# One-hot tiles of the gate stage: two tokens innermost instead of four

## The chip, the cores and the metric

The kernel runs on one core of one Trainium2 chip. The metric is the device time of one execution in microseconds (us), the median of several executions. Five engines work side by side: TensorE (PE, with its weight loads shown apart as PEld), VectorE (DVE), ScalarE (ACT), GpSimd (POOL), and SyncE (SP), which issues most of the DMAs.

## The reference

Two layers of a diffusion backbone over 256 latent and 256 context tokens of width 1024. Each layer has a mixer part (convolution, attention, Hyena, state space) and then an expert layer, PEER, in which every token picks 8 x 16 single-neuron experts out of 128 x 128. The change lies in the expert layer:

```
def peer(h, wq, sub_keys, u_tab, v_tab):
    def block(hb):                                   # 128 tokens
        q = (hb @ wq).reshape(128, 8, 2, 128)
        s = einsum('thpk,hpnk->thpn', q, sub_keys)
        v1, i1 = top_k(s[:, :, 0], 16)
        v2, i2 = top_k(s[:, :, 1], 16)
        cv, ci = top_k(all sums v1 + v2, 16)
        e = i1[ci // 16] * 128 + i2[ci % 16]         # (128, 128) expert numbers
        g = softmax(cv)                              # their gates
        act = gelu(einsum('td,ted->te', hb, u_tab[e]))
        return einsum('te,ted->td', g * act, v_tab[e])
```

## The kernel before

The expert layer is computed densely. All 16384 experts stand in 128 blocks of 128. For each block, `u_stage` (lines 1006 to 1019) loads 512 KB of `u`, splits it on ACT (`u_hi`, line 137) and on POOL or DVE (`u_lo`, line 138) into a rounded part and a rest, multiplies the two with the tokens on PE in 24 matmuls (`au`, lines 141 to 143), and ACT takes the gelu. Later the result is multiplied by gates and goes into the matmuls with `v` (`ov`). In layer 0 three tiles of 128 tokens go this dense way (so `au` has 384 columns) and a fourth is gathered; in layer 1 there are two (256 columns).

The gates come from the gate stage (lines 1170 to 1231). For a token it makes the 128 x 128 table of gates of all experts. The 128 slots of a token (8 heads x 16) lie on the partitions; `slots` brings the slot numbers and gates into that layout, 16 bit wide (`slT`). `hots` makes for a whole tile of 128 tokens the one-hot rows of the upper part of the first index (`o16[0]`, 16 wide), of its lower part (`o8`, 8 wide), and `o16[1]`, `o16[2]`, which are `o16[0]` times the high and the low part of the gate. `gates` then takes 16 tokens at a time (TB = 16, eight calls for a tile, called blocks below): three DVE operations of 2048 elements make `Ah` and `Al` (products of `o16` and `o8`, line 1206) and `B_` (one-hot of the second index, line 1209); two PE matmuls for each token, 128 x 128 x 128 in 16 bit, add `B_` x `Ah` and `B_` x `Al` in PSUM (`G`, lines 1215 and 1216); ACT copies four tokens at a time into `stg`; and SP writes the 16 tables, 1 MB, to DRAM (`Gd`).

In all these 16-bit tiles the last axis is a group of TC = 4 tokens. So `B_` is laid out as (group, 128 classes, 4 tokens), and the matmul of a token reads its 128 numbers at a step of TC elements:

```
o16 = [mk(tp, [128, NG, 16, TC], F16, tag=f"o16{j}", bufs=1) for j in range(3)]      # NG = 128 // TC
Ah = mk(tp, [128, ng, 128, TC], F16, tag="Ah", bufs=2)                               # ng = TB // TC
V.tensor_tensor(dst_.rearrange("p g (a b) c -> p g a b c", b=8), o16[j][:, gs_, :, None, :].to_broadcast(sh),
                o8[:, gs_, None, :, :].to_broadcast(sh), ALU.mult)
V.tensor_tensor(B_, iE[:, None].to_broadcast([128, ng, 128, TC]), ids_[:, :, None, :].to_broadcast([128, ng, 128, TC]), ALU.is_equal)
T.matmul(b[:, j * 128:(j + 1) * 128], B_[:, tt // TC, :, tt % TC], Ah[:, tt // TC, :, tt % TC], start=True, stop=False)
```

`iE` is a constant 0..127, each number TC times, loaded once for each layer. `Ah`, `Al` and `B_` have two buffers each, so the DVE work of block n+2 waits for the matmuls of block n.

Between the blocks PE does `u_stage`s ahead of need: in layer 0 after blocks 0, 2, 4, 6 and 7 of a tile, in layer 1 after every block; their `u_lo` runs on POOL. A scheduler places the instructions when the program is built; each engine then runs its own list in order. There are 24 blocks in layer 0 and 16 in layer 1.

Of the kernel before, what the change touches and what calls it, by code (L numbers as in the profile page):

```python
# [54 lines left out]
UEV = (0, 0)  # L55
GB = 8
TB = 16
TC = 4
GSC = 4096.0

SM = {}
# [22 lines left out]
def tile_hybrid_diffusion(ctx: ExitStack, tc: tile.TileContext, I: dict, out: bass.AP):  # L84
# [12 lines left out]
    def mk(p, shape, dt=F32, tag=None, name=None, **k):  # L97
        uid[0] += 1
        n = f"{name or tag}_{uid[0]}"
        if tag in SCR:  # L100
            k["bufs"] = SCR[tag]
        return p.tile(shape, dt, tag=tag or n, name=n, **k)
# [740 lines left out]
    for l in range(2):  # L843
# [177 lines left out]
        with ExitStack() as rt:  # L1021
# [139 lines left out]
            for t in GT:  # L1161
# [7 lines left out]
                gsl[t] = (eu, gd)  # L1169
            iE = mk(tp, [128, 128, TC], F16, tag="iE", bufs=1)  # L1170
            nc.sync.dma_start(iE, I["iotaE"])
# [10 lines left out]
            def hots(slT):  # L1182
                NG = 128 // TC

                def tv4(j, n):
                    return slT[:, j].rearrange("p (g c) -> p g c", c=TC)[:, :, None, :].to_broadcast([128, NG, n, TC])

                def ids(n):
                    return iE[:, None, 0:n, :].to_broadcast([128, NG, n, TC])
                o16 = [mk(tp, [128, NG, 16, TC], F16, tag=f"o16{j}", bufs=1) for j in range(3)]  # L1190
                o8 = mk(tp, [128, NG, 8, TC], F16, tag="o8", bufs=1)
                for dst_, n, j in ((o16[0], 16, 0), (o8, 8, 1)):
                    V.tensor_tensor(dst_, ids(n), tv4(j, n), ALU.is_equal)
                for j in range(2):
                    V.tensor_tensor(o16[1 + j], o16[0], tv4(3 + j, 16), ALU.mult)
                return slT, o16, o8
# [332 lines left out]
```

## Time and profile before

| | us |
|---|---|
| median of 3 runs | 2989.35 (2978.24 to 2992.91) |
| the profiled execution's own time | 2991.8 |
| its span, first to last instruction | 2990.0 |
| first matmul of the gate stage of layer 0 to its last, about | 652 to 807 |
| the same of layer 1, about | 2246 to 2352 |

PE is busy for 91% of the span, DVE for 69%, ACT for 39%, POOL for 25%. The gate stages take 261 us of the span. In the rows below a line of the trace has the start in us, the duration in us, the engine, the line of the program, the operation, output<-inputs with their shape, and, in brackets, the idle time of the engine before it and what ended that.

### The profile page before, as it was taken

What the parts mean: (1) busy time and instruction counts of PE and PEld (TensorE: products, weight loads), DVE (VectorE), ACT (ScalarE), POOL (GpSimd) and SP (SyncE); (2) the same over time, 40 slices, a digit from 0 to 9 for tenths busy, and PEclk for the clock granted to TensorE, in tenths of its full rate; (3) what the DMA queues carried; (4) which work ended last, traced back from release to release, by engine and by line L of the source; (5) the groups of instructions that cost most, each with busy time, mean ns of one, the idle gap of its engine ahead of it and who ended that gap; (6) DMA issues with size and microseconds to landing.
All of it is one profiled execution on the core that took longest, in us unless ns stands there. A gap on an engine that the chain in (4) does not pass through costs nothing.

```text
span 2990.0 us, 41926 instructions
## 1 busy us (share of the span) xinstructions
PE 2721.2 (91%) x15646; PEld 2352.7 (79%) x15646; DVE 2058.4 (69%) x4255; ACT 1179.0 (39%) x1810; POOL 754.3 (25%) x505
## 2 busy tenths in 40 slices
PE   6798879689999999999989998888779999999998
PEld 3674657489989988888878887666779999999986
DVE  4955449976487777777667646964997665555556
ACT  2233433235433333333333334334345544444443
POOL 2332013032224444444334103321563100000000
PEclk9899989889999999999999998898899999999999
DMA  7123434335699899889989645425336886666655
GB/s 257 56 90 101 140 113 144 128 111 217 230 340 317 312 321 317 305 311 310 310 288 310 215 127 171 129 71 190 113 119 212 288 271 214 217 202 215 203 183 197
DMA packets 241840, 625.21 MB, mean 209 GB/s; under 512 B 22424, under 2 KB 104794, under 8 KB 236004
## 3 DMA queue, kind: packets, MB, share of 16 engines
q1 hardware_dynamic: 201156, 475.18, 48.1%
q0 software_dynamic: 40480, 147.36, 14.0%
q8 instruction: 122, 2.00, 0.3%
q14 instruction: 82, 0.67, 0.1%
HBM read 573.17 MB, written 49.30 MB: 208 GB/s over the span
## 4 chain that ended last, share of the span: by engine, by line
PE 53%; DVE 17%; DMA 13%; issue 9%; POOL 5%; ACT 2%; SPq 0%; POOLq 0%; DVEq 0%; ACTq 0%
DMA grow<-in_vg_dram,eu 9%; PE ov L141 6%; PE ov L142 6%; PE ov L143 6%; PE au L141 5%; PE au L143 5%; PE au L142 5%; POOL grow L1311 4%; PE G L1215 3%; PE G L1216 3%; DVE yT L365 2%; PE pj L141 1%; DVE accg L1324 1%; PE pj L142 1%; PE pj L143 1%
## 5 line engine op out<-in xcount | busy, mean ns | idle before, releaser
L141 PE MATMUL au<-hT,u_hi 128*128 128x384 f32 (+1 forms) x2048 | 642.5, 314 | 3.6 <-ACT u_hi L137 3.6
L143 PE MATMUL au<-hT,u_lo 128*128 128x384 f32 (+1 forms) x2048 | 639.7, 313 | 4.5 <-POOL u_lo L138 3.2
L142 PE MATMUL au<-hT,u_hi 128*128 128x384 f32 (+1 forms) x2048 | 638.9, 312 | 0.0
L142 PE MATMUL ov<-v_lo,wh 128*128 128x512 f32 x1280 | 506.0, 395 | 32.7 <-DVE v_lo L138 32.6
L143 PE MATMUL ov<-v_hi,wl 128*128 128x512 f32 x1280 | 500.7, 391 | 0.0
L141 PE MATMUL ov<-v_hi,wh 128*128 128x512 f32 x1280 | 463.5, 393 | 6.2 <-ACT wh L137 6.2
L137 ACT CAST u_hi<-u_raw 128x1024 fp32r<-128x1024 f32 x256 | 269.6, 1053 | 487.0 <-PE au L142 364.3
L141 PEld LDWEIGHTS au<-hT,u_hi 128*128 128x128 f32 x2048 | 392.5, 192 | 12.2 <-ACT u_hi L137 4.5
L142 PEld LDWEIGHTS au<-hT,u_hi 128*128 128x128 f32 x2048 | 391.8, 191 | 7.7
L143 PEld LDWEIGHTS au<-hT,u_lo 128*128 128x128 f32 x2048 | 391.0, 191 | 8.0 <-POOL u_lo L138 3.9
L138 DVE TENSOR_TENSOR v_lo<-v_raw,v_hi 128x1024 fp32r<-128x1024 f32 x255 | 313.0, 1228 | 79.6 <-ACT v_hi L137 79.5
L138 DVE TENSOR_TENSOR u_lo<-u_raw,u_hi 128x1024 fp32r<-128x1024 f32 x198 | 242.3, 1224 | 159.7 <-ACT u_hi L137 159.7
L137 ACT CAST v_hi<-v_raw 128x1024 fp32r<-128x1024 f32 x256 | 268.8, 1050 | 137.6 <-DMA v_raw<-in_v_dram 103.7
L142 PEld LDWEIGHTS ov<-v_lo,wh 128*128 128x128 f32 x1280 | 241.9, 189 | 89.4 <-DVE v_lo L138 45.5
L137 ACT CAST wh<-act 128x384 fp32r<-128x384 f32 (+1 forms) x256 | 117.4, 461 | 447.1 <-PE ov L142 446.1
L141 PEld LDWEIGHTS ov<-v_hi,wh 128*128 128x128 f32 x1280 | 242.4, 190 | 51.3 <-ACT wh L137 6.5
L143 PEld LDWEIGHTS ov<-v_hi,wl 128*128 128x128 f32 x1280 | 242.1, 189 | 49.9
L138 POOL TENSOR_TENSOR w_lo<-w_raw,w_hi 128x1024 fp32r<-128x1024 f32 (+1 forms) x72 | 177.8, 2478 | 252.7 <-ACT w_hi L137 221.8
L1311 POOL DMA_INDIRECT grow<-in_vg_dram,eu x128 | 175.0, 1367 | 230.2 <-DVE accg L1324 187.1
L1311 POOL DMA_INDIRECT grow<-in_ug_dram,eu x128 | 161.2, 1260 | 272.4 <-DVE grow L1315 222.1
L138 POOL TENSOR_TENSOR u_lo<-u_raw,u_hi 128x1024 fp32r<-128x1024 f32 x58 | 149.6, 2585 | 305.0 <-ACT u_hi L137 240.8
L1324 DVE SCALAR_TENSOR_TENSOR accg<-grow,ag,accg 128x1024 f32<-128x1024 f32 x127 | 163.0, 1283 | 83.0 <-DMA grow<-in_vg_dram,eu 82.5
(832 smaller groups left out, 4493.3 us busy)
## 6 DMA issues: line engine op xcount, KB each, us to landing
u_raw<-in_uT_dram SPq DMA_DIRECT2D x256, 512.0 KB
v_raw<-in_v_dram SPq DMA_DIRECT2D x256, 512.0 KB
Gd<-stg SPq DMA_DIRECT2D x40, 1024.0 KB
gt<-Gd SPq DMA_DIRECT2D x80, 512.0 KB
wa_raw<-in_w_ada_dram SPq DMA_DIRECT2D x76, 512.0 KB
w_raw<-in_w_in_t_dram SPq DMA_DIRECT2D x44, 512.0 KB
w_raw<-in_wq_dram SPq DMA_DIRECT2D x32, 512.0 KB
w_raw<-in_w_ada_dram SPq DMA_DIRECT2D x20, 512.0 KB
```

Of the source, the lines that this page charges most:

```text
L137: S.copy(hi, src)
L138: late["V" if eng in (None, V) else "G"] = (eng or V).tensor_tensor(lo, src, hi.bitcast(F32), ALU.subtract)
L141: T.matmul(o, lh, rh, start=first, stop=False)
L142: T.matmul(o, lh, rl, start=False, stop=False)
L143: return T.matmul(o, ll, rh, start=False, stop=last)
L365: V.scalar_tensor_tensor(uc, upad[:, m, :, j:j + 256], wj, uc, op0=ALU.mult, op1=ALU.add)
L1215: T.matmul(b[:, j * 128:(j + 1) * 128], B_[:, tt // TC, :, tt % TC], Ah[:, tt // TC, :, tt % TC], start=True, stop=False)
L1216: T.matmul(b[:, j * 128:(j + 1) * 128], B_[:, tt // TC, :, tt % TC], Al[:, tt // TC, :, tt % TC], start=False, stop=True)
L1311: nc.gpsimd.indirect_dma_start(out=r, out_offset=None, in_=I[tab], in_offset=bass.IndirectOffsetOnAxis(ap=eu[:, i:i + 1], axis=0))
L1324: V.scalar_tensor_tensor(accg, r, ag[:, i:i + 1], accg, op0=ALU.mult, op1=ALU.add)
```

## The change

One constant is set from 4 to 2:

```
-TC = 4
+TC = 2
```

With it the last axis of `iE`, `o16`, `o8`, `Ah`, `Al` and `B_` is 2 tokens long, and the axis of groups is twice as long: `Ah` goes from (4, 128, 4) to (8, 128, 2) in each partition. The number of instructions, their elements, the buffers and their bytes stay, but for `iE`, which is half as long (64 KB to load instead of 128 KB). The order of the instructions is the same on PE, DVE, ACT and POOL, and on SP but for the size of the two loads of `iE`. What changes is how the data lie: a matmul of the gate stage reads its 16-bit numbers 4 bytes apart instead of 8, both for the weights (`B_`) and for the moving side (`Ah`, `Al`); and a DVE operation that repeats tokens along an axis reads a run of 2 numbers (4 bytes) again and again, where it read a run of 4 (8 bytes).

## Rows read from the trace of the kernel before

**Rows 1.** Both gate stages: length, busy us (and count) of PE, PEld, DVE, ACT, POOL, clock, DMA.

```profile
652.00:807.00 155.00, 154.97 (x1138) 150.87 (x1138) 89.02 (x79) 79.44 (x132) 36.59 (x15) 1.00 0.59 212
2246.00:2352.00 106.00, 106.00 (x882) 104.45 (x882) 65.33 (x52) 57.13 (x96) 32.49 (x13) 0.98 0.64 222
```

**Rows 2.** PE in order of time, layer 1: a gate block, a `u_stage`, the next block.

```profile
2274.71 0.30 PE L1216 MATMUL G<-Al,B__3362_19163 128*128 128x128 f16 x1
...
2278.02 0.30 PE L1216 MATMUL G<-Al,B__3362_19163 128*128 128x128 f16 x1
...
2278.27 0.28 PE L142 MATMUL au<-hT,u_hi 128*128 128x256 f32 x1
...
2280.91 0.28 PE L143 MATMUL au<-hT,u_lo 128*128 128x256 f32 x1
2281.03 0.29 PE L1215 MATMUL G<-Ah,B__3375_19244 128*128 128x128 f16 x1
```

**Rows 3.** PE in order of time, layer 0: matmuls of a `u_stage`.

```profile
672.18 0.34 PE L142 MATMUL au<-hT,u_hi 128*128 128x384 f32 x1
...
673.40 0.34 PE L143 MATMUL au<-hT,u_lo 128*128 128x384 f32 x1
```

**Rows 4.** Weight loads and matmuls in order of time; last, all transposes of one line.

```profile
657.67 0.12 PEld L1215 LDWEIGHTS <-B__857_4886 128*128 128x128 f16 x1 [0.15 <-issue]
657.68 0.13 PEld L1216 LDWEIGHTS <-B__857_4886 128*128 128x128 f16 x1
...
671.43 0.30 PE L1216 MATMUL G<-Al,B__878_5015 128*128 128x128 f16 x1
671.54 0.62 PE L1175 MATMUL tr<-cm,sl 128*128 128x128 f32 x4
...
L789 PE MATMUL xT<-cm,grow x8: 270/272/273, 1797.2 to 1798.0; 128*128 128x128 f32 x8
```

**Rows 5.** POOL and DVE in order of time, layer 1, around one block.

```profile
2282.28 2.39 POOL L138 TENSOR_TENSOR u_lo<-u_raw,u_hi 128x1024 fp32r<-128x1024 f32 x1 [4.26 <-ACT u_hi L137]
...
2284.91 1.23 DVE L1206 TENSOR_TENSOR Ah<-o,o 128x2048 f16<-128x2048 f16 x1 [3.18 <-PE G L1215]
2286.06 1.22 DVE L1206 TENSOR_TENSOR Al<-o,o 128x2048 f16<-128x2048 f16 x1
2287.19 1.22 DVE L1209 TENSOR_TENSOR B__3401_19406<-iE,slT 128x2048 f16<-128x2048 f16 x1
```

**Rows 6.** POOL and DVE in order of time, layer 0, where both want to run.

```profile
635.83 3.06 POOL L138 TENSOR_TENSOR u_lo<-u_raw,u_hi 128x1024 fp32r<-128x1024 f32 x1 [2.02 <-ACT u_hi L137]
...
636.75 3.22 DVE L1209 TENSOR_TENSOR B__870_4967<-iE,slT 128x2048 f16<-128x2048 f16 x1
...
648.59 2.58 POOL L138 TENSOR_TENSOR u_lo<-u_raw,u_hi 128x1024 fp32r<-128x1024 f32 x1 [1.89 <-ACT u_hi L137]
...
648.84 3.41 DVE L1206 TENSOR_TENSOR Al<-o,o 128x2048 f16<-128x2048 f16 x1
```

**Rows 7.** Waits in layer 0's gate stage, then in layer 1's: total us, times, longest.

```profile
DVE Ah L1206 <- PE G L1215: 58.5, 20, 6.5
...
DVE Ah L1206 <- PE G L1215: 32.8, 11, 4.0
```

**Rows 8.** DVE in order of time: sums in 16 bit, runs of 8, 4, 2 elements.

```profile
487.67 0.67 DVE L1067 TENSOR_TENSOR e<-e 128x1024 f16<-128x1024 f16 x1
...
510.25 0.44 DVE L1067 TENSOR_TENSOR e<-e 128x512 f16<-128x512 f16 x1
...
511.64 0.43 DVE L1067 TENSOR_TENSOR e<-e 128x256 f16<-128x256 f16 x1
```

**Rows 9.** DVE products in 32 bit by line: duration ns min/median/max.

```profile
L618 DVE TENSOR_TENSOR t2k<-t2k,cbm x12: 665/693/831, 222.3 to 1993.9; 128x512 f32<-128x512 f32 x12
...
L619 DVE TENSOR_TENSOR t2k<-t2k,dt x12: 677/692/743, 223.2 to 1994.6; 128x512 f32<-128x512 f32 x12
```

**Rows 10.** The stretch behind the gate stage of layer 0, columns as in rows 1.

```profile
807.00:860.00 53.00, 46.77 (x237) 43.33 (x237) 39.19 (x109) 17.66 (x26) 11.64 (x9) 0.94 1.00 331
```

## Prediction

> **What bounds the kernel now.** I read the busy shares by stage first, then PE's instructions in order of time, then DVE and POOL in the same stretches. In both gate stages PE is busy from end to end, 154.97 of 155 us and 106 of 106, and DVE and POOL are not [rows 1]. DVE waits there for the gate matmuls that free its buffers, 58.5 and 32.8 us in all [rows 7]. So PE sets the length of both stages, and its work is of two kinds. A gate matmul follows the one before after 0.118 us: 28 steps from 2274.71 to 2278.02. An `au` matmul of 256 columns takes 0.120 us: 22 steps from 2278.27 to 2280.91 [rows 2]. One of 384 columns takes 0.174 us: 7 steps in 1.22 us [rows 3]. A block is thus 32 x 0.118 = 3.78 us of gate matmuls, and a `u_stage` 24 x 0.120 = 2.88 us in layer 1 and 24 x 0.174 = 4.18 us in layer 0. Layer 1 has 16 x (3.78 + 2.88) = 106.6 us, which is the stage; layer 0 has 24 x 3.78 + 15 x 4.18 = 153.4 us, which is nearly the stage.
>
> **The change on PE.** The reader should note that a gate matmul has 128 columns and takes as long as an `au` of 256. From 256 to 384 columns the price rises by 0.054 us, 0.42 ns a column, so 128 columns at that rate would cost 0.120 - 0.054 = 0.066 us. The weight load doesn't explain the rest: with PE just free, the second load of a block starts 0.01 us behind the first, and the transposes behind a block, which have loads of another kind, still start 0.11 us after the last gate matmul [rows 4]. It is the matmul itself that occupies the array for 0.118 us. What sets it apart from `au` is its moving side: 16-bit numbers 8 bytes apart, where `au` reads 32-bit numbers that touch, 4 bytes apart. The change puts the 16-bit numbers 4 bytes apart, at the very addresses that `au` reads at 0.42 ns a column. The trace shows no 16-bit matmul at another step, so the price has bounds: 0.066 us below, 0.118 us above, since the numbers only move closer together. A row between is the transposes of 128 columns in 32 bit, 0.11 us (8 starts from 1797.2 to 1798.0 [rows 4]), but those are another type of matmul. I take 0.066, because the addresses are those of `au`. That is 32 x 0.052 = 1.66 us less for a block, 40 us for 24 blocks and 27 us for 16: PE's own work would fall to 115 us and 79 us.
>
> [...]
>
> **DVE.** Its operations keep their elements. Today 2048 elements in 16 bit take 1.22 us and start 1.14 us apart [rows 5]. Two elements are done at a time there: 512 elements in 32 bit take 0.69 us [rows 9], so a 32-bit word costs about (1.22 - 0.69) / 512 = 1.04 ns, and 1024 words of two numbers each fit 1.22 us. After the change a run is exactly one such word, and one input repeats that word, up to 128 times, while the other input and the output stay contiguous. Two rows bound this. Line 619 repeats one 32-bit word 128 times over 512 elements and takes 0.692 us, as line 618, which repeats whole rows, takes 0.693 [rows 9]: repeating a word is free. Against it, line 1067 needs 0.44 us for 512 elements in runs of four and 0.43 us for 256 in runs of two [rows 8]: there runs of two go at half the rate. But in that line both inputs and the output jump after each run; here nothing jumps. I take 1.14 us as before and keep half the rate, 1.22 + 1024 x 1.04 ns = 2.28 us, 2.20 from start to start, for a rival.
>
> [...]
>
> **What is late next.** PE can't collect the whole 67 us, because DVE and POOL do not run their two-input operations at the same time. A POOL `u_lo` begins at 635.83 and lasts 3.06 us; a DVE operation begins at 636.75 and takes 3.22 us instead of 1.22; the same at 648.59 and 648.84 [rows 6]. DVE ended each time some 1.1 us behind POOL: it had waited for the whole of it. Today the two take turns without loss in layer 1: POOL runs from 2282.28 for 2.39 us, while PE does a block, and DVE's three operations follow at 2284.91, when the block ends and PE turns to `u_stage` [rows 5]. With shorter blocks the two stand in a row. Their sum in layer 0: DVE 89.0 us less 0.08 us of overlap for each of 79 records, 82.7, and POOL 36.6, together 119.3 us [rows 1]; behind the last DVE operation PE has still two blocks and a `u_stage`, 2 x 2.1 + 4.2 = 8.4 us. That is 127.7 us, above PE's 115, so the stage goes from 155 to about 128: **27.3 us** saved. In layer 1: 65.3 - 52 x 0.08 = 61.1, POOL 32.5, and 2 x 2.1 + 2.9 = 7.1 behind: 100.7 us, above PE's 79, so the stage goes from 106 to about 101: **5.3 us** saved. Some of the recorded DVE time is itself waiting for POOL, which makes these sums a little long; new stalls in changing over make them short. I leave both out.
>
> The rest costs nothing. ACT has 79.4 and 57.1 us in the stages [rows 1], under either sum. The DMAs move 212 GB/s there and would move 212 x 155 / 128 = 257, below the 331 GB/s of the next stretch [rows 10]. That stretch has its DMA share at 1.00, but it begins with loads of the gate tables, which must be written first, so it moves forward as a whole. The shorter load of `iE` lies ahead of its use. Sum: 2991.8 - 27.3 - 5.3 = 2959.2, say **2959 us**; against the median of 2989.35, which is 2.5 us below the profiled execution, that is 1.0% faster.
>
> **The rivals.** *PE's step stays at 0.118 us*, because the step of 8 bytes was not its cause. Then PE bounds the stages as now: 2990, give or take 5. For it speaks that no 16-bit row at another step exists. A weaker form of it is a step of 0.11, as in the transposes: 40 x 32 x 0.008 = 10 us saved, 2980. *DVE drops to half rate.* The place is the three operations of a block, the price 2.20 us for 1.14, a factor of 1.93: layer 0 then has 82.7 x 1.93 + 36.6 + 8.4 = 205 us for 155, layer 1 61.1 x 1.93 + 32.5 + 7.1 = 158 for 106, so 102 us more: 3094. [...] *DVE and POOL get out of each other's way* better than their sum says; then PE's own work bounds: 2991.8 - 67 = 2925. Against it stand the collisions of rows 6.
>
> **How the numbers follow.** A measurement of this kernel can tell about 0.5%, 15 us, from no change. Chances: the forecast, 2947 to 2972, 0.55; the step unchanged or nearly so, 2980 to 2995, 0.27; less collision, 2925 to 2945, 0.06; DVE slower, 3040 to 3100, 0.12. Faster by over 0.5% is the first and third, 0.61; within 0.5% the second, 0.27; slower the last, 0.12. The range runs from 2940 to 2996, which leaves out the slower case and most of the third; the forecast's own range is 2947 to 2972.
>
> **What would show it.** Right: starts of gate matmuls 0.066 us apart in a block (up to 0.08 changes little), DVE operations at 1.22 us, idle time of PE inside the gate stages that ends with `Ah`, `Al` or `B_`, more DVE records of 2 to 3.4 us beside a `u_lo`, stages of about 128 and 101 us, and everything behind them as long as before. Wrong: gate matmuls still 0.118 apart, or DVE operations of 1.9 us or more. A granted clock below the 1.00 and 0.98 of the stages [rows 1], brought by the new idle time of PE, would eat some of the gain.

## The result and the profile after

The changed kernel takes **2945.15 us** (median of 4 runs, 2932.18 to 2949.5), the kernel before beside it 2987.64 (4 runs, 2978.24 to 2992.91). The ratio is 0.9854 with a 95% interval of 0.9813 to 0.9895: 42.5 us or 1.5% faster, where 30 us were forecast. The time lies in the range on record, 2940 to 2996, and 2 us below the forecast's own range of 2947 to 2972. A second measurement against 13 runs of the kernel before (the first experiment below) gives 0.9853, from 0.983 to 0.9876.

The windows of both gate stages of after, in the columns of [rows 1]:

```profile
652.00:783.00 131.00, 114.30 (x1136) 109.66 (x1134) 108.20 (x79) 70.32 (x130) 56.20 (x15) 0.96 0.68 244
2214.50:2306.00 91.50, 80.17 (x879) 77.69 (x879) 85.33 (x52) 51.67 (x94) 35.91 (x13) 0.94 0.70 241
```

The stages went from 155 to 131 us and from 106 to 91.5. PE's busy time fell by 41 and 26 us, but PE is no longer busy from end to end: 17 and 11 us are idle. Its granted clock fell too, from 1.00 and 0.98 to 0.96 and 0.94. DVE and POOL together are recorded for 164 us in a stage of 131, against 126 in 155 before. Since no work was added to either, the growth of their records is waiting for one another.

PE in order of time in layer 1, at the place of [rows 2], a gate block, a `u_stage` and the next block:

```profile
2250.18 0.23 PE L1215 MATMUL G<-Ah,B__3388_19325 128*128 128x128 f16 x1 [0.66 <-DVE B__3388_19325 L1209]
...
2251.96 0.22 PE L1216 MATMUL G<-Al,B__3388_19325 128*128 128x128 f16 x1
...
2252.19 0.28 PE L142 MATMUL au<-hT,u_hi 128*128 128x256 f32 x1
...
2254.82 0.28 PE L143 MATMUL au<-hT,u_lo 128*128 128x256 f32 x1
2255.79 0.23 PE L1215 MATMUL G<-Ah,B__3401_19406 128*128 128x128 f16 x1 [0.68 <-DVE B__3401_19406 L1209]
```

From the first of the 32 gate matmuls to the last it is 1.78 us, 31 steps of **0.057 us**, where it was 0.118. The `au` matmuls are as before: 22 steps in 2.63 us. And both blocks now begin with a wait for DVE's `B_`, 0.66 and 0.68 us: PE waits for DVE where DVE waited for PE.

DVE, POOL, PE and ACT of after in order of time, where layer 0 goes from its second tile of tokens to its third (the record of 724.37 holds two operations):

```profile
720.96 1.21 DVE L1209 TENSOR_TENSOR B__1009_5800<-iE,slT 128x2048 f16<-128x2048 f16 x1
722.10 1.21 DVE L1206 TENSOR_TENSOR Ah<-o,o 128x2048 f16<-128x2048 f16 x1
...
724.37 18.84 POOL L138 TENSOR_TENSOR u_lo<-u_raw,u_hi 128x1024 fp32r<-128x1024 f32 x2 [6.87 <-ACT u_hi L137]
...
728.91 1.21 DVE L1195 TENSOR_TENSOR o<-o,slT 128x2048 f16<-128x2048 f16 x1
...
737.46 1.22 DVE L1209 TENSOR_TENSOR B__1060_6099<-iE,slT 128x2048 f16<-128x2048 f16 x1
...
740.93 0.69 PE L143 MATMUL au<-hT,u_lo 128*128 128x384 f32 x1 [6.74 <-POOL u_lo L138]
...
746.69 1.05 ACT L137 CAST u_hi<-u_raw 128x1024 fp32r<-128x1024 f32 x1 [11.46 <-PE au L142]
747.82 2.40 POOL L138 TENSOR_TENSOR u_lo<-u_raw,u_hi 128x1024 fp32r<-128x1024 f32 x1 [4.62 <-ACT u_hi L137]
750.78 1.23 DVE L1206 TENSOR_TENSOR Ah<-o,o 128x2048 f16<-128x2048 f16 x1 [12.10 <-PE G L1215]
```

DVE's operations last 1.21 us and start 1.14 us apart, as in [rows 5]: the one-word runs cost DVE nothing. The long POOL record is the new thing. DVE runs without a gap from 715 to 738.7 us, and two `u_lo` that take 2.4 us each when alone are recorded for 18.8: the first for 16.5, of which all but the last 2.2 lie beside DVE's run, the second for 2.4. In a1, the second measurement of this kernel, POOL's 15 records in the stage again hold 54.27 us, against 56.20 here and 36.59 before. An `au` matmul waits 6.7 us for the first of them. The gate blocks stand behind it in PE's order, so the buffers that they free come late, and DVE stands for 12.1 us. The collisions of [rows 6] went the other way, DVE waiting for POOL; here POOL waits for DVE.

The waits of after, in layer 0's gate stage and then in layer 1's, answering to [rows 7]:

```profile
DVE Ah L1206 <- PE G L1215: 20.4, 5, 12.1
PEld au L143 <- POOL u_lo L138: 7.0, 1, 7.0
PE au L143 <- POOL u_lo L138: 6.7, 1, 6.7
...
PE G L1215 <- DVE Ah L1206: 12.1, 2, 7.5
...
DVE Ah L1206 <- PE G L1215: 4.7, 2, 3.0
```

DVE's waits for a gate matmul fell from 58.5 to 20.4 and from 32.8 to 4.7 us, and 12.1 of the 20.4 is the one just shown. Of PE's 12.1 us of waiting for `Ah` in layer 1, 7.5 stand before the first gate matmul, in the kernel before as well.

**Where the 43 us are.** The table gives, for every kernel of this study, the time from the start of the first gate matmul to the start of the last in either stage, worked out from the traces, with the stretch between the stages and the tail behind the second. "Step" is the median distance of two gate matmuls' starts (in e9, where two distances alternate, the mean).

```
kernel                    time us   step us  layer 0  between  layer 1   tail
before                    2991.8*    0.118     154.4   1439.6    105.3  638.8
after                     2945.15    0.057     130.9   1431.8     91.1  640.9
a1  after, again          2945.54    0.057     131.1   1439.6     90.2  640.2
e1  weights in twos       2986.05    0.117     153.1   1434.6    104.5  639.6
e2  moving in twos        2959.98    0.060     132.6   1440.3     91.4  640.7
e3  eight tokens          3177.55    0.234     265.9   1428.9    186.8  642.2
e4  one token             3080.73    0.056     208.0   1433.8    137.0  639.7
e5  after, u_lo on DVE    2908.24    0.057     117.2   1428.3     78.5  640.0
e6  before, u_lo on DVE   2973.08    0.118     155.2   1414.2    105.4  639.1
e7  e5, lead-in on DVE    2904.09    0.057     113.6   1418.9     76.0  640.3
e8  6 bytes apart         2984.44    0.088     156.6   1427.0    107.8  640.5
e9  Ah 8, Al 4 apart      2947.82    0.088     132.2   1432.8     93.4  638.9
(* the profiled execution; elsewhere the median of several runs, and one run each for e1 to e4, e8 and e9;
the stages are those of the profiled execution everywhere)
```

In the first profile of after the stages give 23.5 and 14.2 us and the stretch between them another 7.8. In the second (a1) the stages give 23.3 and 15.1, and the stretch between them is 1439.6 us, exactly as before. That stretch differs by some 13 us among kernels that all keep `u_lo` on POOL (1427.0 to 1440.3), in no order that follows the stages. So the change itself gives 38 us in the gate stages; the 8 us of the first profile did not come again in the second and are not counted as its work.

### The profile page after: what moved, and what is told of

Same layout as the page of the kernel before. It is cut to its first block, busy times and chain, and to the rows that moved or that the text cites. A ratio compares the mean times of both kernels' runs of the same rounds, so it can differ in the third digit from the quotient of the medians.

```text
span 2946.4 us, 41926 instructions
## 1 busy us (share of the span) xinstructions
PE 2656.8 (90%) x15646; PEld 2286.7 (78%) x15646; DVE 2099.5 (71%) x4255; ACT 1164.1 (40%) x1810; POOL 778.3 (26%) x505
## 4 chain that ended last, share of the span: by engine, by line
PE 46%; DVE 20%; DMA 14%; issue 12%; POOL 5%; ACT 3%; SPq 0%; POOLq 0%; DVEq 0%; ACTq 0%
DMA grow<-in_vg_dram,eu 8%; PE ov L142 6%; PE ov L141 6%; PE ov L143 5%; POOL grow L1311 5%; PE au L141 4%; PE au L143 4%; PE au L142 4%; DVE yT L365 2%; PE pj L141 1%; PE pj L142 1%; PE pj L143 1%; DMA wa_raw<-in_w_ada_dram 1%; DVE accg L1324 1%; DVE e L1067 1%
## 5 line engine op out<-in xcount | busy, mean ns | idle before, releaser
L138 POOL TENSOR_TENSOR u_lo<-u_raw,u_hi 128x1024 fp32r<-128x1024 f32 x58 | 171.4, 2961 | 257.3 <-ACT u_hi L137 250.8
```

The costliest lines, as they stand in the source:

```text
L138: late["V" if eng in (None, V) else "G"] = (eng or V).tensor_tensor(lo, src, hi.bitcast(F32), ALU.subtract)
```

## The experiments

**The change measured again**, beside the two kernels that move `u_lo`.

> The changed kernel once more, timed beside the kernel before on the chip of the next two runs: 0.985 of it, 2945, within 8.

Measured: 2945.54 us (2938.42 to 2952.55), the kernel before 2985.03 (13 runs); ratio 0.9853, from 0.983 to 0.9876.

**Which side of the matmul: the weights.** Only `B_`, which the array takes as weights, gets runs of two; `Ah` and `Al`, the moving side, keep four. `B_` is compared with a constant tile of its own for that, loaded beside `iE`.

```diff
-TC = 4
+TC, TW = 4, 2
-                B_ = mk(tp, [128, ng, 128, TC], F16, tag="B_", bufs=2)
+                B_ = mk(tp, [128, nw, 128, TW], F16, tag="B_", bufs=2)
```

> Only B_, the weights of the gate matmuls, is laid out with 2 tokens innermost (its own constant iW); Ah and Al keep 4. If the moving side's step sets the matmul's time, the gate matmuls stay 0.118 us apart and the time stays at the kernel before's, 2988, within 10. If the step of the weights sets it, they come 0.057 us apart and the time is that of the changed kernel, 2945.

Measured: 2986.05 us, with 2977.57 for the kernel before beside it, one run each. A line of the group view, the 16 matmuls of one block with `Ah` (duration ns min/median/max, first and last start):

```profile
L1215 PE MATMUL G<-Ah,B__879_5017 x16: 296/297/297, 668.3 to 671.8; 128*128 128x128 f16 x16
```

15 pairs take 3.5 us, 0.117 us a matmul, as before. With the moving side 8 bytes apart, bringing the weights together gains nothing.

**Which side of the matmul: the moving side.** The other half: `Ah` and `Al` in twos, `B_` in fours.

```diff
-TC = 4
+TC, TW = 2, 4
-                B_ = mk(tp, [128, ng, 128, TC], F16, tag="B_", bufs=2)
+                B_ = mk(tp, [128, nw, 128, TW], F16, tag="B_", bufs=2)
```

> Only Ah and Al, the moving side of the gate matmuls, have 2 tokens innermost; B_ keeps 4. If the moving side's step sets the matmul's time: 0.057 us apart and 2945, within 10. If the weights' step sets it: 0.118 us and 2988. If both must be at 4 bytes: 0.118 us here and with the weights alone.

Measured: 2959.98 us in one run. The same group of this kernel, and its two stages in the columns of [rows 1]:

```profile
L1215 PE MATMUL G<-Ah,B__879_5017 x16: 218/221/225, 665.6 to 667.4; 128*128 128x128 f16 x16
```

```profile
653.00:786.00 133.00, 116.50 (x1137) 111.78 (x1136) 109.05 (x79) 70.98 (x130) 56.29 (x15) 0.96 0.68 246
2226.00:2318.00 92.00, 81.28 (x880) 78.87 (x880) 85.56 (x53) 51.87 (x95) 36.07 (x13) 0.94 0.70 242
```

15 pairs in 1.8 us, 0.060 us a matmul, and stages within 2 us of after's. All of the effect but 0.003 us a matmul comes from the moving side. The time is 12 us above after's profiled execution of 2948.2, but of these only some 2 us lie in the gate stages; 8.5 are in the stretch between them, which is as long as in a1.

**The step of the moving side doubled.** Eight tokens innermost: the numbers 16 bytes apart.

```diff
-TC = 4
+TC = 8
```

> TC = 8 for all: a step of 16 bytes. If PE takes the moving side in pieces of 8 bytes, one piece for each number already at a step of 8, the gate matmuls stay 0.118 us apart and the time is 2988. [...]

Measured: 3177.55 us in one run. The block's group, then windows over that block's predecessor and the block itself:

```profile
L1215 PE MATMUL G<-Ah,B__878_5015 x16: 411/414/422, 678.4 to 685.4; 128*128 128x128 f16 x16
```

```profile
671.00:678.00 7.00, 7.00 (x32) 4.38 (x32) 0.00 (x0) 3.17 (x5) 2.39 (x1) 0.86 0.08 32
678.30:685.50 7.20, 7.20 (x33) 4.45 (x32) 3.50 (x3) 2.39 (x4) 0.00 (x0) 0.50 0.64 218
```

15 pairs take 7.0 us, 0.233 us a matmul: twice the price of 8 bytes, and not the 0.118 us expected of pieces of 8 bytes. It is not the clock that makes it: at a granted clock of 0.86 and of 0.50 a block takes the same 7 us. But the low clock reaches what comes behind: the `au` matmuls after this block start 0.32 us apart for three microseconds, until 689.6 (granted clock 0.50 from 686 to 688), and 0.174 from there on.

**The step halved once more.** One token innermost: the numbers touch, 2 bytes apart, and DVE's repeated run is a single 16-bit number.

```diff
-TC = 4
+TC = 1
```

> TC = 1 for all: 16-bit numbers that touch, a step of 2 bytes, and DVE operations in which one input repeats a single 16-bit number. The gate matmuls should stay 0.057 us apart (128 columns at 0.42 ns are 0.053). DVE should lose its pairs: 2.28 us for an operation of 2048 where it is 1.22, so that DVE and POOL set both stages, 205 us and 158 us by the sums of the prediction, 3080 in all. If DVE keeps its rate, the time is that of the changed kernel, 2945.

Measured: 3080.73 us in one run. One block's group on PE at a granted clock of 1.00 and one at 0.50, and DVE in order of time:

```profile
L1215 PE MATMUL G<-Ah,B__893_5105 x16: 219/219/231, 687.9 to 689.6; 128*128 128x128 f16 x16
...
L1215 PE MATMUL G<-Ah,B__878_5015 x16: 289/314/314, 678.6 to 681.8; 128*128 128x128 f16 x16
```

```profile
685.06 2.28 DVE L1206 TENSOR_TENSOR Ah<-o,o 128x2048 f16<-128x2048 f16 x1
687.26 2.28 DVE L1206 TENSOR_TENSOR Al<-o,o 128x2048 f16<-128x2048 f16 x1
689.46 4.43 DVE L1209 TENSOR_TENSOR B__901_5153<-iE,slT 128x2048 f16<-128x2048 f16 x1
```

PE gains nothing at 2 bytes over 4: 0.057 us again, which is the end of this saving. DVE goes to 2.28 us, 2.20 from start to start, the half rate that the prediction had priced as a rival. That rival is real, but here it comes with runs of one number and not with runs of two, which took 1.21 us. (The third operation, 4.43 us, lies beside a `u_lo` of POOL.) The stages are 208 and 137 us. The slower block, 0.107 us a matmul, is one at a granted clock of 0.50 (its window from 678.60), and it began after 4.5 us in which PE waited for `B_`.

**POOL's work taken away, in the new kernel.** In the loop between the blocks `u_lo` goes to DVE, so that POOL has nothing to do in the gate stages.

```diff
-                            u_stage(bl, G)
+                            u_stage(bl, V)
```

> The changed kernel, with the u_lo of the u_stages between the blocks on DVE instead of POOL. If DVE and POOL taking turns set the stages now, this shortens them: a u_lo holds DVE for 1.14 us where POOL kept both for 2.4 or more, so DVE alone has 79 x 1.14 + 15 x 1.14 = 107 us in layer 0 and 52 x 1.14 + 13 x 1.14 = 74 in layer 1, and PE's own work, 24 x 1.82 + 15 x 4.18 = 106 and 16 x 1.82 + 16 x 2.88 = 75, sets them: 115 and 83 us with the ends, where they are 131 and 91; 24 us less in all, 2921. If something else holds PE back there (DMA, ACT, the matmuls), the time stays at 2945 or rises, since DVE gets more work.

Measured: 2908.24 us (2902.22 to 2914.3); ratio to before 0.973, from 0.9707 to 0.9752. Its stages in the columns of [rows 1], and one of its `u_lo` in order of time:

```profile
648.50:766.00 117.50, 112.80 (x1138) 109.74 (x1137) 103.60 (x94) 70.44 (x130) 0.00 (x0) 0.97 0.75 277
2194.00:2272.50 78.50, 74.78 (x875) 73.27 (x875) 75.36 (x68) 50.56 (x94) 0.00 (x0) 1.00 0.85 305
```

```profile
660.14 1.23 DVE L138 TENSOR_TENSOR u_lo<-u_raw,u_hi 128x1024 fp32r<-128x1024 f32 x1 [0.67 <-ACT u_hi L137]
```

DVE got more work, and both stages got shorter, by 14 and 13 us. A `u_lo` costs 1.23 us on DVE; on POOL it costs 2.4 us, and DVE's two-input operations beside it waited for its end, 3.22 and 3.41 us for 1.22 [rows 6]. PE is busy for 112.8 of 117.5 and 74.8 of 78.5 us: the stages are close to PE's own work again. This kernel and e7, below, are the only ones whose slowest run is faster than every run of both kernels; the expectation of 2921 was 13 us too high.

**The same in the kernel before.**

```diff
-                            u_stage(bl, G)
+                            u_stage(bl, V)
```

> The kernel before with the same move of u_lo to DVE. PE's own work fills its stages, 155 and 106 us, so nothing is to be gained: 2988, within 8, unless DVE's longer row delays the blocks.

Measured: 2973.08 us (10 runs, 2963.75 to 2981.22); ratio 0.9962, from 0.9949 to 0.9975. Its stages:

```profile
648.00:803.00 155.00, 154.69 (x1134) 150.21 (x1133) 106.20 (x94) 78.83 (x131) 0.00 (x0) 1.00 0.57 211
2217.30:2323.00 105.70, 104.57 (x877) 102.62 (x877) 78.07 (x69) 56.71 (x96) 0.00 (x0) 1.00 0.68 235
```

The stages don't move, 155.2 and 105.4 us by first and last start, for 154.4 and 105.3: with PE busy for 154.7 of 155.0 and 104.6 of 105.7 us, POOL's work was hidden. What this kernel does gain, 12 us, lies outside: its first gate matmul comes 4 us sooner, and the profiled execution, at 2963.75 us the fastest of its ten, has a stretch between the stages of 1414 us, the shortest of all. Why is open; the move changes the order on PE, DVE, ACT and POOL.

**The lead-in too.** e5, with the `u_lo` ahead of the first block on DVE as well.

```diff
-UEV = (0, 0)
+UEV = (1, 1)
```

> The best version so far (two-token tiles, u_lo between the blocks on DVE) with the u_lo in the lead-in of both gate stages on DVE too, in place of POOL. There, in layer 0 from 632 to 648 us, four DVE groups of two last 4.55 us instead of 2.35 beside a POOL u_lo. Theory (DVE waits for the whole of a POOL u_lo, 2.4 us, which costs 1.14 us on DVE itself): some four u_lo give back 1.2 us each, the first gate matmul comes about 4 to 5 us sooner in layer 0 and up to as much in layer 1, so about 2900 us for 2908. Rival (the lead-in is bound by what feeds it, the selection's chain on DVE, and u_lo on DVE gets in its way): 2908 or up to 2915.

Measured: 2904.09 us (2901.78 to 2906.67); ratio to before 0.9746, from 0.9729 to 0.9762, whose interval overlaps that of e5: no measurable difference. A pair of products beside POOL's `u_lo` in e5, then the same kind in e7:

```profile
641.05 4.55 DVE L1206 TENSOR_TENSOR Ah<-o,o 128x2048 f16<-128x2048 f16 x2
```

```profile
640.79 2.36 DVE L1206 TENSOR_TENSOR Ah<-o,o 128x2048 f16<-128x2048 f16 x2
```

The collision is gone, as the theory says, and yet the first gate matmul comes at 651.1 us instead of 648.5. The stage behind it is 3.6 us shorter in return, and layer 1's is 2.5 us shorter. So in layer 0 the theory was right on the price and wrong on the place: the products were not what the first gate matmul waited for. In both kernels PE comes to it straight from `au` matmuls, without idle time, and its `Ah` had been ready for 4 us or more.

**A step between, 6 bytes.** After's tiles, but each run of two in `Ah` and `Al` takes three places.

```diff
-TC = 2
+TC, TP = 2, 3
-                Ah = mk(tp, [128, ng, 128, TC], F16, tag="Ah", bufs=2)
-                Al = mk(tp, [128, ng, 128, TC], F16, tag="Al", bufs=2)
+                Ah = mk(tp, [128, ng, 128, TP], F16, tag="Ah", bufs=2)
+                Al = mk(tp, [128, ng, 128, TP], F16, tag="Al", bufs=2)
...
-                    V.tensor_tensor(dst_.rearrange("p g (a b) c -> p g a b c", b=8), o16[j]...
+                    V.tensor_tensor(dst_.rearrange("p g (a b) c -> p g a b c", b=8)[:, :, :, :, 0:TC], o16[j]...
```

> After's tiles with one part changed: Ah and Al keep runs of two tokens, but each run now takes three places, so that the moving side's numbers lie 6 bytes apart instead of 4. Everything else, B_ included, is as in after. The moving side's price so far is 0.057 us a gate matmul at 2 and at 4 bytes, 0.118 at 8, 0.234 at 16. Theory 'in proportion to the step above 4 bytes': 6 bytes give 0.118 x 6/8 = 0.088 us, a block of 2.8 us. Rival 'whole units of 4 bytes': 0.118 us, the block as long as in the kernel before (3.65 us from its first start to its last). On DVE the output now jumps by 2 bytes after each pair of numbers. Theory of the prediction (only a repeated word is free; a jump behind each run costs): Ah and Al go from 1.21 to about 2.28 us each. Rival 'the output's step is free as well': 1.21 us. With both at 2.28 the sum of DVE in layer 0 grows by 48 x 1.06 = 51 us and the stage from 131 to about 180 us; with both at 1.21 it stays between 131 and 155.

Measured: 2984.44 us in one run. The block on PE, and DVE in order of time:

```profile
L1215 PE MATMUL G<-Ah,B__878_5015 x16: 247/250/253, 666.6 to 669.2; 128*128 128x128 f16 x16
```

```profile
685.61 1.90 DVE L1206 TENSOR_TENSOR Ah<-o,o 128x2048 f16<-128x2048 f16 x1
687.35 1.90 DVE L1206 TENSOR_TENSOR Al<-o,o 128x2048 f16<-128x2048 f16 x1
```

15 pairs in 2.6 us, 0.087 us a matmul: in proportion to the step (0.088 expected), not in whole words. DVE fell between the theories, 1.90 us. Every second of its output words now lies off the 4-byte grid. With DVE slower, the stages are back at 156.6 and 107.8 us although PE's matmuls are a quarter cheaper than before. PE is busy for 138.1 and 93.3 us of them, DVE and POOL are recorded for 143.4 and 46.6 in the first and 103.9 and 44.0 in the second: DVE and POOL bound them.

**Two steps side by side.** `Ah` in runs of two that take four places (8 bytes), `Al` dense (4 bytes).

```diff
-TC = 2
+TC, TP = 2, 4
-                Ah = mk(tp, [128, ng, 128, TC], F16, tag="Ah", bufs=2)
+                Ah = mk(tp, [128, ng, 128, TP], F16, tag="Ah", bufs=2)
```

> After's tiles, but Ah alone in runs of two tokens that take four places: its numbers lie 8 bytes apart on the moving side and its words lie 8 bytes apart in DVE's output, while Al stays dense. Each kernel of this form has both kinds side by side, in alternate gate matmuls and alternate DVE operations. Theory (the moving side's step alone sets the price of a gate matmul): those with Ah occupy 0.118 us, those with Al 0.057, so a block's steps alternate and it lasts about 32 x 0.0875 = 2.8 us. Rival (something else of the four-token tile was dear): all at 0.057. On DVE: theory of the prediction (a jump behind each pair halves the rate) Ah 2.28 us beside Al at 1.21; rival (jumps of the output by whole 4-byte words are free) both 1.21. At 2.28 the stage of layer 0 goes from 131 to about 131 + 24 x 1.06 = 156 us, that of layer 1 from 91 to about 108, the time to about 2990; at 1.21 to about 2950 to 2960.

Measured: 2947.82 us in one run. The block on PE, its stages, and DVE in order of time:

```profile
L1215 PE MATMUL G<-Ah,B__878_5015 x16: 276/276/278, 662.9 to 665.5; 128*128 128x128 f16 x16
```

```profile
648.60:781.00 132.40, 132.21 (x1137) 129.23 (x1135) 96.51 (x79) 75.32 (x131) 39.38 (x15) 1.00 0.69 247
2213.60:2307.20 93.60, 91.66 (x877) 90.41 (x876) 86.40 (x53) 53.49 (x95) 38.88 (x13) 0.97 0.71 245
```

```profile
677.17 1.21 DVE L1206 TENSOR_TENSOR Ah<-o,o 128x2048 f16<-128x2048 f16 x1
678.30 1.21 DVE L1206 TENSOR_TENSOR Al<-o,o 128x2048 f16<-128x2048 f16 x1
```

2.6 us for 15 pairs: on average 0.087 us, half way between 0.057 and 0.118, as the theory of the moving side's step says. The single steps don't split cleanly into 0.057 and 0.118: they are 0.09 us behind a matmul with `Ah` and 0.07 to 0.09 behind one with `Al`, so the two prices are seen only in their mean. On DVE the output that jumps by a whole word costs nothing, 1.21 us, against the theory. And the kernel takes the same time as after, though its PE works 18 and 11 us more in the stages: PE is just full here, at a granted clock of 1.00 and 0.97. This puts the crossing near 0.088 us. What the gate matmul saves below that, after does not collect: its PE stands idle for 17 and 11 us, and its granted clock is 0.96 and 0.94.

## Why the prediction was right, and where it was off

**What bounds the stages: right.** e6 shows it from the other side: with POOL's work gone the stages of before did not move, 155.2 and 105.4 us for 154.4 and 105.3.

**The moving side's step is the price: right.** e1 and e2 separate it from the weights, and five steps give one line: 0.057 us at 2 and 4 bytes, 0.087 at 6, 0.118 at 8, 0.234 at 16, which above 4 bytes is 0.0146 us a byte for 128 numbers. At 8 bytes the gate matmul costs twice what it costs at 4, and at 16 bytes four times. The term was mis-sized on the cautious side, 0.066 taken and 0.057 measured, below the lower bound. The bound came from the distance between 256 and 384 columns of 32-bit numbers, 0.42 ns a column, taken off 0.120 us, which leaves a fixed 0.012 us in every matmul; the 0.057 us of the gate matmul have room for 0.003. Simply halving the `au` row would have given 0.060. A saving of 0.061 us is 47 us for 768 matmuls and 31 us for 512. PE's busy time fell by only 41 and 26; that this agrees with the 40 and 27 worked out is luck, because the lower granted clock, 0.96 and 0.94 for 1.00 and 0.98, took part of the saving back. The size had no measurable effect on the time: e9, at 0.088, takes as long in its one run.

**DVE keeps its rate: right, one reason too many.** 1.21 us after, 1.22 before. That repeating a word is free was the reason that carries. That nothing may jump was not needed: e9's output jumps by 8 bytes and costs nothing, 1.21 us. The chance of 0.12 for the slower rival was not idle, since e4 hits its price, 2.28 us, with runs one number shorter, and e8 comes to 1.90 us with pairs 6 bytes apart in the output. The 1.9 us from which an operation was to count as wrong, and the 3040 us at which the range of the slower case begins, were the author's estimate: no run shows 1.9 us for a repeated pair with a dense output. The runs show 1.21 us for it.

**What is late next: the right mechanism, both sums off.** The forecast was 128 and 101 us, the windows show 131 and 91.5. By the records of after, DVE or POOL or both are at work for 119.3 us of the first window and neither for 11.7; in the second it is 86.1 and 5.4. The prediction had 119.3 + 8.4 and 93.6 + 7.1.

That the two work one after the other is borne out by e5, which has no POOL in the stages and shows DVE's work alone: 103.6 us less 15 `u_lo` of 1.22 is 85.3, and 75.4 less 16 is 55.8. With 15 and 13 `u_lo` of 2.39 us on POOL [rows 5] that makes 121.2 and 86.9 us, against the 119.3 and 86.1 of after.

In layer 1 this term of the sum was 7.5 us too big. It took DVE's records of before, 65.3 us, as work, and left out that they contain waiting for POOL. Three of the 52 records hold about 6 us of it; two of them:

```profile
2255.59 3.42 DVE L1209 TENSOR_TENSOR B__3334_18992<-iE,slT 128x2048 f16<-128x2048 f16 x1
2295.68 3.43 DVE L1206 TENSOR_TENSOR Al<-o,o 128x2048 f16<-128x2048 f16 x1
```

So DVE and POOL did not take turns without loss in layer 1 even before. POOL's 32.5 us contain another 1.4.

In layer 0 the term is right to the tenth, and that is luck. For each record the prediction took 0.08 us of overlap off the busy time, 6.3 us in layer 0 and 4.2 in layer 1. But the busy time of a window counts an overlap only once to begin with. A window of the kernel before with the three operations of [rows 5], DVE alone:

```profile
2284.50:2288.32 3.82, 3.41 (x3) 1.00 0.56 210
```

Inside it the three records last 3.58 us one by one; the busy time is the 3.41 from the first start to the window's end. Without the second deduction the sums would have been 134.0 and 104.9 us, a gain of 22 us instead of 33.

The time in which neither engine works was mis-sized too. The last DVE operation of the gate stage ends 2.8 us before the last gate matmul starts, 3.2 us in layer 1, where 8.4 and 7.1 had been taken: PE, which now waits for DVE, is no longer two blocks behind. In layer 0 the pauses inside the stage make up for that and more; 2.5 us of them stand at 655.6 (3.2 in the kernel before), 4.6 at 743.2 and 1.8 at 772.4. The one at 743.2 belongs to the "new stalls in changing over" that were left out: from the end of the long POOL record to the next `u_lo` at 747.8 neither engine works, because PE has first to catch up with what waited for POOL. It does so in part at a granted clock of 0.50. The clock was still 1.00 from 734 to 738, where PE was busy for 0.19 of 4 us, and lower behind that:

```profile
738.00:744.80 6.80, 3.87 (x12) 3.87 (x13) 0.68 (x1) 0.00 (x0) 5.20 (x2) 0.50 0.42 113
```

In this window the `au` matmuls start 0.32 us apart; behind it, at 1.00 up to 750.6, 0.174. e5, where nothing has to wait for POOL, is without this pause. The lower clock that the prediction named as a danger thus came, and took some of the gain.

So both omissions that the prediction named were real: the waiting made layer 1's sum too long, the stalls made layer 0's too short, and the double deduction shortened both. The gain of the stages, 38 us where 33 were forecast, is close in part by luck. Taken off the median of the kernel before in the same measurement, 2987.6, it gives about 2950; the 5 us from there to 2945 are within the spread of the runs.

**What follows moves forward whole: right.** In a1 the stretch between is as long as before to a tenth of a microsecond (in the first profile it was 7.8 us shorter); the tail is 638.8 us before and 640 to 641 after.

**The rivals.** PE's step unchanged and DVE at half rate did not come, and each could be produced, by e1 (0.117 us) and by e4 (2.28 us). "DVE and POOL get out of each other's way", 2925, did not come either, and e5 shows what it would take: one of the two must give up its work. Its stages, 117.2 and 78.5 us, come to the 115 and 79 that this rival had. That the time is 2908 and not 2925 is due to what lies outside them: in its profile the stretch between the stages is 11 us shorter than in the kernel before and the first gate matmul comes 3.5 us sooner. Why is open, as in e6.

## What to carry to other kernels

Look at the distance in bytes between successive numbers of a matmul's moving side: for 128 numbers of 16 bit 2 and 4 bytes cost the same here, 0.057 us, and above that the price rose in proportion, to 0.118 at 8 and 0.234 at 16; weights 4 bytes apart did not help while the moving side stayed at 8 (0.117 in e1). Before collecting such a saving, add up what the engines that feed PE must do one after the other, DVE and POOL above all, and take their work from a stretch in which they don't collide, since a record beside a collision contains waiting (3.2 to 3.4 us for 1.22 here). The busy time of a window already counts overlaps once (3.41 us for records of 3.58). When the feeders become the bound, moving POOL's two-input operations onto DVE can shorten a stage though DVE is the busier engine: by 14 and 13 us in e5.

## What the runs showed of the hardware

- A gate matmul of 128 columns costs 0.057 us with the moving numbers 2 or 4 bytes apart, 0.087 at 6, 0.118 at 8 and 0.234 at 16. At 16 bytes the price is the same at a granted clock of 0.86 and of 0.50; at 2 bytes it goes from 0.057 to 0.107 us at 0.50.
- The granted clock fell to 0.50 in a block of matmuls 16 bytes apart (e3, 678.30 to 685.50) although PE is recorded as busy for all 7.20 us; the stages of that kernel have a mean of 0.70 and 0.71. In the kernel before, with reads 8 bytes apart and PE busy for 154.97 of 155 us and 106 of 106, it was 1.00 and 0.98.
- DVE, 2048 numbers in 16 bit: 1.21 us with a repeated pair of numbers, also when the output's pairs lie 8 bytes apart; 1.90 when they lie 6 bytes apart; 2.28 when a single number is repeated.
- A DVE that ran without a gap, from 715 to 738.7 us, kept POOL waiting: a `u_lo` that takes 2.4 us alone was recorded for 16.5 us. In both profiles of after POOL's 15 records of layer 0's stage hold 54 to 56 us, where 36.6 stood before.
